# Product order, the steps of an attention pair, and who empties a plain bank, in a two-layer hybrid model

## The chip, the cores and the metric

The kernel runs on one core of one Trainium2 chip. The metric is the device time of one execution in microseconds, as the median of several runs. A core has five engines that matter here: PE (TensorE, matmuls into the eight PSUM banks), DVE (VectorE), ACT (ScalarE), POOL (GpSimd) and SP (SyncE, which here only issues DMAs). POOL too is used mostly to issue DMAs. Each engine works through its own instructions in their order, and waits for the others by semaphores.

## The reference, cut to what matters

512 tokens of width 1024 pass through two layers: dilated attention and a gated feed-forward block, then an mLSTM mixer and another feed-forward block. Only the attention is touched. It has three groups of query, key and value projections with 8 heads of 128; each group attends within windows of its own dilation, and the groups are joined by a softmax over their log-sums.

```python
proj = (xn @ w_in).reshape(B, S, N_GROUPS, 3, ATTN_HEADS, ATTN_HEAD_DIM)
for g, (window, dilation) in enumerate(((128, 1), (512, 4), (2048, 16))):
    q = apply_partial_rope(proj[:, :, g, 0], positions) * scale
    k = apply_partial_rope(proj[:, :, g, 1], positions)
    o, lse = dilated_window_attention(q, k, proj[:, :, g, 2], window, dilation)
wts = jax.nn.softmax(jnp.stack(lses), axis=0)
o = jnp.einsum('gbsh,gbshd->bshd', wts, jnp.stack(outs))
h = h + o.reshape(B, S, ATTN_WIDTH) @ w_out
```

## The kernel before, in words

All matmuls of projections are made in float32 by three products of rounded parts: an operand is split into a high part (ACT, `split_chunk`, L213) and a remainder (DVE subtraction, L214), and high times high, high times low and low times high are added up in a bank. A weight chunk of 128 x 1024 elements is loaded by SP into one of three raw buffers (`wraw`), split into one of four pairs of split buffers, and used by PE. `Feed` hands out the chunks in the order of a list, `plan`, and prepares three chunks ahead of the one that is being multiplied.

The heads are worked off in four **pairs**, pr = 0 to 3. While PE projects queries and keys of pair pr (`project_pair`), the attention of the pair before is done beside it. The names in the trace carry the pair first: a1g2 is group 2 of pair 1.

For pairs 1 to 3, group 0 is projected **plainly**: two chunks for the queries, two for the keys, each into two banks; `evac` (L948 to L961) empties a bank, with two ACT instructions that pack the 32 rows that rotation needs (L959) and a third that copies the whole bank (L961). For pair 0 the whole bank is emptied by DVE, which multiplies by the norm's factor (L952), and ACT packs from the copy (L956).

Groups 1 and 2 are projected together for queries and keys by a Strassen scheme (`qk_unit`): seven **products** P1 to P7 of half the size, each of 24 matmuls of 128 x 256, in the order of `ORDER`, which is also the order of the values in an earlier stage. They share three banks: P1 and P2 add up in c11, P5 and P3 in p5, and P6, P7 and P4 in u. After P1, ACT copies c11 into u (L878), and P6 adds to that. After P5 and after P6, ACT copies their bank into `vu` (L881, L883); P7 may add to u only when P6's copy has been taken. After P7 and P3, DVE adds bank and `vu` to the keys (L896); P4 may add to u only after P7's addition has read it. After P2 and P4, ACT packs and copies (L872, L890). P5, P6 and P7 need weight differences, which DVE makes (L845) in `prepare_part`; that function also starts the loads of the next group's weight quarters W11, W12, W21 and W22. After P4 the rotation of the group follows: a shuffle and three DVE passes (L593 to L602), and ACT copies back (L608 or L610), in group 1 one step later.

**Steps.** `advance` counts steps and runs what was put off until then (`defer`). Group 0 of a pair makes four steps (one for each chunk); each Strassen group makes four more, after its 2nd, 4th, 6th and 7th product. So in a pair steps 5 to 8 lie in group 1 and steps 9 to 12 in group 2. `RUN_AT` says at which steps of a pair the attention of the pair before is run:

```python
SCORES0_AT = 5
RUN_AT = (1, (4, 5, 6, 7, 8), (10, 11), (2, 3, 1))
```

- step 1: scores of groups 1 and 2 (`scores12`, L707) and their exponentials (L732);
- step 4: joint softmax factors and the first head's weighing (L777, L780), run in the middle of the last plain chunk;
- step 5: the first head's 32 x 32 transposition on DVE (L786) and its four stores to DRAM from POOL's queue (L789);
- step 6: the second head's weighing; step 7: its transposition and stores, and the first head's read-back (`bring`, L794, POOL's queue); step 8: the second head's read-back;
- steps 10 and 11: the two heads' weighted **values** (L804, L809), 30 matmuls each into one bank, which ACT copies (`keep_head`, L622) and POOL stores;
- steps 2, 3 and 1: the loads of the values from DRAM.

`SCORES0_AT` counts from the end of group 0 (step 4): so at step 9 the **first scores** of the new pair (`scores0`, L686) are computed, into two banks with the tag "s" for the first head and two with the tag "o" for the second; DVE adds the mask and takes the maxima (L692), which empties the banks, then exponentials follow on ACT (L726). Values needs a bank with the tag "o" as well, of which there are two. The probabilities and their transposed copies share four buffers (tag "p").

**What sets the order.** The framework plans each engine's order ahead of the run: an instruction traced earlier has priority, but one that the planner takes to be ready may pass another that it takes to be waiting. `run` keeps a block of matmuls together behind the PE instruction traced last and lets later ones follow it; `tc.issue_after(ins)` keeps all instructions of its block behind `ins` on that engine. Neither adds a semaphore.

Of the kernel before, what the change touches and what calls it, by code (L numbers as in the profile page):

```python
# [11 lines left out]
F32 = mybir.dt.float32  # L12
# [3 lines left out]
ALU = mybir.AluOpType  # L16
# [16 lines left out]
C1 = 6.28125  # L33
C2 = float(np.float32(np.uint32(np.float32(TWO_PI - C1).view(np.uint32) & 0xFFFFF000).view(np.float32)))
C3 = float(np.float32(TWO_PI - C1 - C2))
SCORES0_AT = 5
RUN_AT = (1, (4, 5, 6, 7, 8), (10, 11), (2, 3, 1))
LAST_AT = (1, (3, 3, 3, 3, 3), (), (1, 1, 1))
STACK_AT = (9, 11, 15, 17)
HEAD_AT = ((9, 10, 12), (10, 11, 13), (12, 13, 15), (13, 14, 16), (15, 16, 18), (16, 17, 19), (18, 19, 21),  # L40
# [33 lines left out]
def tile_hybrid_dilated_attn_mlstm(  # L74
# [127 lines left out]
        return raw, n, view, name  # L202

    spare = []
    splits = itertools.count()

    def split_chunk(chunk):

        raw, n, view, name = chunk
        p, more, bufs = (spare[0], "4", 1) if spare and next(splits) % (W_BUFS + 1) == W_BUFS else (wp, "", W_BUFS)  # L210
        hi = p.tile([P, 1024], F32R, tag="whi" + more, name=name + "_h", bufs=bufs)
        lo = p.tile([P, 1024], F32R, tag="wlo" + more, name=name + "_l", bufs=bufs)
        nc.scalar.activation(hi[:, :n], raw[:, :n], AF.Copy)  # L213
        nc.vector.tensor_tensor(lo[:, :n], raw[:, :n], hi[:, :n].bitcast(F32), op=ALU.subtract)  # L214
        return view(hi), view(lo)

    def split_weights(src, shape, name):
# [172 lines left out]
    with ExitStack() as actx:  # L390
# [249 lines left out]
        def attention_pair(pr, qks):  # L640
# [36 lines left out]
            def scores0(q, k):  # L677

                for i in range(2):
                    for b2 in range(2):  # L680
                        sp = score_bank(i, "%ss0" % nm)
                        o, parts = 0, []
                        for b in (2 * b2, 2 * b2 + 1):
                            lo_ = max(b - 1, 0) * P
                            w = (b + 1) * P - lo_
                            nc.tensor.matmul(sp[:, o:o + w], q[:, i, b * P:(b + 1) * P],  # L686
                                             k[:, i, lo_:lo_ + w], start=True, stop=True)
                            parts.append((b, o, w))
                            o += w
                        for b, o, w in parts:  # L690
                            pb = max(2 * b - 1, 0)
                            nc.vector.tensor_tensor_reduce(  # L692
                                p0[i][:, pb:pb + w // P, :].rearrange("p a b -> p (a b)"),
                                sp[:, o:o + w], mask_band[:, 2 * P - w:], 1.0, -3e38,
                                op0=ALU.add, op1=ALU.max, accum_out=own[:, 0, 0, i, b:b + 1])
                for i in range(2):
                    exponentials(0, i)

# [127 lines left out]

        postponed = []

        four_k = lambda t: t.rearrange("p (k n) -> p k n", k=4)
        parts_of = {}  # L830

# [9 lines left out]
        def prepare_part(pr, g, name):  # L841
            b = parts_of[pr, g]

            def less(out, x, y):
                nc.vector.tensor_tensor(b[out], b[x], b[y], op=ALU.subtract)  # L845
            src = {"P1": "W11", "P5": "W11", "P6": "W11", "P2": "W21", "P7": "W12", "P3": "W22", "P4": "W21"}[name]
            if name == "P5":
                less("W11", "W12", "W11")
            elif name == "P6":
                less("W11", "W22", "W11")  # L850
            elif name == "P7":
                less("W12", "W22", "W12")
            whl = split_chunk((b[src], 1024, four_k, "a%dg%d%s" % (pr, g, name)))
            if name == "P7":
                less("W21", "W21", "W11")
                for key in ("W11", "W12"):
                    load_part(pr, g + 1, key)
            elif name == "P4":
                for key in ("W21", "W22"):
                    load_part(pr, g + 1, key)  # L860
            return whl

        def qk_unit(pr, g, qk):
# [10 lines left out]
            def finish(name):  # L874
                nonlocal rot, vu
                if name == "P1":
                    acc["u"] = acc_tile(nm + "u")
                    nc.scalar.activation(acc["u"], acc["c11"], AF.Copy)  # L878
                elif name == "P5":
                    vu = ap.tile([P, 2, SEQ], F32, tag="vu", name=nm + "vu")  # L880
                    nc.scalar.activation(vu[:, 0], acc["p5"], AF.Copy)  # L881
                elif name == "P6":
                    nc.scalar.activation(vu[:, 1], acc["u"], AF.Copy)  # L883
                elif name in ("P2", "P4"):
                    th = int(name == "P4")
                    src = two_m(acc[target[name]])
                    if th == 0:
                        rot = ap.tile([P, 2, SEQ], F32, tag="rot", name="rot")
                    pack(th, src[:R])
                    nc.scalar.activation(halves(qk[0], th), src, AF.Copy)  # L890
                    if last and th:
                        rope(qk, rot, False, 1, 2, True)
                else:
                    th = int(name == "P7")
                    out = halves(qk[1], th)
                    nc.vector.tensor_tensor(out, two_m(acc[target[name]]), two_m(vu[:, 1 - th]), op=ALU.add)  # L896
                    pack(2 + th, out[:R])
                    if last and th == 0:
                        rope(qk, rot, False, 0, 1, True)
                        rope(qk, rot, False, 2, 4, True)  # L900

            for n, name in enumerate(ORDER):
                key = target[name]
                if name in ("P1", "P5"):
                    acc[key] = acc_tile(nm + key)
                whl = feed.pop()
                with fenced():
                    for m in range(2):
                        for k in range(4):
                            for a, b in SPLITS:  # L910
                                if name in ("P1", "P2", "P4"):
                                    x_ = pair[b][k + 4 * (name != "P1")][:, HALF * (name == "P4"):HALF * (1 + (name == "P4"))]
                                else:
                                    x_ = sum_part(name, b, k)
                                nc.tensor.matmul(acc[key][:, m * HALF:(m + 1) * HALF], whl[a][:, k, m * P:(m + 1) * P], x_,
                                                 start=(name in ("P1", "P5") and m == 0 and k == 0 and (a, b) == SPLITS[0]),
                                                 stop=(m == 1 and k == 3 and (a, b) == SPLITS[-1]), skip_group_check=True)
                finish(name)
                if n == 6 and not last:
                    back = rope(qk, rot, False)  # L920
                    if g == 2:
                        back()
                    else:
                        defer(1, back)
                if n in (1, 3, 5, 6):
                    advance()

        def project_pair(pr, qks, then=None):
            nm = "a%d" % pr
            for g in range(3):  # L930
# [14 lines left out]
                for part in range(2):  # L945
                    t = tok_tile("%sg%d_%s" % (nm, g, "qk"[part]))

                    def evac(m, acc, t=t, rot=rot, g=g, part=part):  # L948
                        to = rot()
                        views = (in_order, by_block) if g == 0 else (lambda x: x,) * 2  # L950
                        if pr == 0:
                            nc.vector.tensor_tensor(views[0](t[:, m]), views[1](acc), views[1](rbc), op=ALU.mult)  # L952
                        for th in range(2):
                            q = 2 * part + th
                            if pr == 0:
                                nc.scalar.activation(packed(to, q, m, g == 0),  # L956
                                                     turned((t, t), q, m, g == 0), AF.Copy)
                            else:
                                nc.scalar.activation(packed(to, q, m, False), acc[:R, th * HALF:(th + 1) * HALF], AF.Copy)  # L959
                        if pr:  # L960
                            nc.scalar.activation(views[0](t[:, m]), views[1](acc), AF.Copy)  # L961
                    if pr == 0 and g == 0 and part == 0:
                        def first_evac(evac=evac):
                            bc_hook()
# [212 lines left out]

        def last_plain(pr):
            whl = split_chunk(weight_chunk(w_in, 1, pr * 256 + D, 4, "a%dg0k_k1" % pr))
            for key in ("W11", "W12", "W21", "W22"):  # L1180
                load_part(pr, 1, key)
            return whl

# [2 lines left out]
        for pr in range(HEADS // 2):  # L1186
            for g, part, ch in itertools.product(range(3), range(2), range(2)):
                if pr and g:
                    if (part, ch) == (0, 0):
                        plan += [lambda pr=pr, g=g, name=name: prepare_part(pr, g, name) for name in ORDER]  # L1190
                elif pr and (part, ch) == (1, 1):
                    plan.append(lambda pr=pr: last_plain(pr))
                elif (pr, g) != (0, 0):
# [1141 lines left out]
```

## Time and profile before

| | |
|---|---|
| median of 3 runs | 1407.97 us (1407.84 to 1408.24) |
| the profiled execution | 1408.62 us |
| its span, first to last instruction | 1406.8 us |
| granted TensorE clock, mean of the span | 0.994 |
| PE busy | 1377.5 us, 98% |
| DVE busy | 1105.8 us, 79% |
| ACT busy | 803.7 us, 57% |
| PE busy in pair 1, 176.0 to 262.4 | 79.85 of 86.40 us |
| PE busy in pair 2, 262.4 to 344.4 | 79.85 of 82.00 us |
| PE busy in pair 3, 344.4 to 426.9 | 78.23 of 82.50 us |

In the profile, L214 is line 214 of the kernel; `a1g2u<-S3h,a1g2P_h` names what an instruction writes and reads, without buffer numbers. A row of the list of waits reads: who waited, for whom, the total in us, how many times, the longest. A row of the timeline reads: start, duration, engine, line, operation, names, shapes, count, and in brackets the engine's idle time before it and what ended it. A row of the table of stretches reads: the stretch, its length, busy time and instructions of PE, of its weight loads, DVE, ACT and POOL, the granted clock, the DMAs' share and GB/s. A row of the groups ends with busy time, mean ns of one, and idle time before them.

### The profile page before, as it was taken

What the parts mean: (1) busy time and instruction counts of PE and PEld (TensorE: products, weight loads), DVE (VectorE), ACT (ScalarE), POOL (GpSimd) and SP (SyncE); (2) the same over time, 40 slices, a digit from 0 to 9 for tenths busy, and PEclk for the clock granted to TensorE, in tenths of its full rate; (3) what the DMA queues carried; (4) which work ended last, traced back from release to release, by engine and by line L of the source; (5) the groups of instructions that cost most, each with busy time, mean ns of one, the idle gap of its engine ahead of it and who ended that gap; (6) DMA issues with size and microseconds to landing.
All of it is one profiled execution on the core that took longest, in us unless ns stands there. A gap on an engine that the chain in (4) does not pass through costs nothing. (4 is left out here: it accounts for less than half of the span.)

```text
span 1406.8 us, 22647 instructions
## 1 busy us (share of the span) xinstructions
PE 1377.5 (98%) x8740; PEld 1249.7 (89%) x8740; DVE 1105.8 (79%) x1841; ACT 803.7 (57%) x1346; POOL 163.1 (12%) x240
## 2 busy tenths in 40 slices
PE   9999998999999999999999999999999999999997
PEld 7888888899888788999999998888888899999886
DVE  7758668585877289878878888998858987887887
ACT  6556576566765155544466554786534544458854
POOL 3000011111011001000000101113101240001213
PEclk9999999999999999999999999999999999999999
DMA  8534247346275546432354652333334563335963
GB/s 286 181 120 135 92 138 227 121 132 217 65 240 152 170 128 161 132 121 74 107 168 95 145 149 75 93 91 99 97 120 111 131 201 121 120 106 130 199 165 98
DMA packets 140068, 193.82 MB, mean 138 GB/s; under 512 B 8980, under 2 KB 104788, under 8 KB 139960
## 3 DMA queue, kind: packets, MB, share of 16 engines
q1 hardware_dynamic: 119552, 139.81, 31.6%
q0 software_dynamic: 18752, 51.43, 15.9%
q8 instruction: 69, 1.13, 0.3%
q10 hardware_dynamic: 1656, 1.12, 0.2%
q14 instruction: 39, 0.32, 0.1%
HBM read 167.30 MB, written 22.54 MB: 135 GB/s over the span
## 5 line engine op out<-in xcount | busy, mean ns | idle before, releaser
L1638 POOL DMA_DIRECT2D f1T<-in_ffn_w_out_dram x15 | 17.8, 1186 | 208.8 <-DMA f1P_2w_w<-in_ffn_w_out_dram 136.4
L1613 POOL DMA_DIRECT2D f0S<-in_ffn_w_out_dram x10 | 8.7, 874 | 260.2 <-ACT f0P L1595 172.9
L2170 POOL DMA_DIRECT2D hD<-hB x32 | 21.7, 696 | 68.5 <-DVE hB L2167 68.5
L244 PE MATMUL mo<-n_h,mo_k_l 128*128 128x512 f32 x64 | 25.3, 396 | 0.0
L244 PE MATMUL mo<-n_h,mo_k_h 128*128 128x512 f32 x64 | 25.2, 394 | 0.0
L244 PE MATMUL mo<-n_l,mo_k_h 128*128 128x512 f32 x64 | 25.2, 394 | 0.0
L244 PE MATMUL awo<-ao_h,awo_k_h 128*128 128x512 f32 x64 | 25.2, 393 | 0.0
L244 PE MATMUL mwo<-yo_l,mwo_k_h 128*128 128x512 f32 x64 | 25.1, 393 | 0.0
L244 PE MATMUL mqk<-n_h,mqk_k_h 128*128 128x512 f32 x64 | 25.1, 392 | 0.0
L244 PE MATMUL awo<-ao_l,awo_k_h 128*128 128x512 f32 x64 | 25.1, 392 | 0.0
L244 PE MATMUL mqk<-n_l,mqk_k_h 128*128 128x512 f32 x64 | 25.1, 392 | 0.0
L244 PE MATMUL f0j<-n_h,f0j_h 128*128 128x512 f32 x64 | 25.0, 391 | 0.0
L244 PE MATMUL f1j<-n_h,f1j_h 128*128 128x512 f32 x64 | 25.0, 391 | 0.0
L244 PE MATMUL mwo<-yo_h,mwo_k_l 128*128 128x512 f32 x64 | 25.0, 391 | 0.0
L244 PE MATMUL mqk<-n_h,mqk_k_l 128*128 128x512 f32 x64 | 25.0, 390 | 0.0
L244 PE MATMUL awo<-ao_h,awo_k_l 128*128 128x512 f32 x64 | 25.0, 390 | 0.0
L244 PE MATMUL f0j<-n_h,f0j_l 128*128 128x512 f32 x64 | 24.9, 390 | 0.0
L244 PE MATMUL f1j<-n_h,f1j_l 128*128 128x512 f32 x64 | 24.9, 390 | 0.0
L244 PE MATMUL f0j<-n_l,f0j_h 128*128 128x512 f32 x64 | 24.9, 389 | 0.0
L244 PE MATMUL f1j<-n_l,f1j_h 128*128 128x512 f32 x64 | 24.9, 389 | 0.0
L244 PE MATMUL mwo<-yo_h,mwo_k_h 128*128 128x512 f32 x64 | 24.8, 391 | 0.0
L214 DVE TENSOR_TENSOR v1P_l<-v1W,v1P_h 128x1024 fp32r<-128x1024 f32 x14 | 17.1, 1223 | 9.3 <-ACT v1P_h L213 9.3
(2617 smaller groups left out, 5896.0 us busy)
## 6 DMA issues: line engine op xcount, KB each, us to landing
f0j_w<-in_ffn_w_in_dram SPq DMA_DIRECT2D x17, 512.0 KB, 5.9
f1j_w<-in_ffn_w_in_dram SPq DMA_DIRECT2D x17, 512.0 KB, 6.0
f1T<-in_ffn_w_out_dram POOLq DMA_DIRECT2D x15, 512.0 KB, 7.4
f0hid<-in_ffn_w_in_dram SPq DMA_DIRECT2D x9, 512.0 KB, 5.8
f1hid<-in_ffn_w_in_dram SPq DMA_DIRECT2D x9, 512.0 KB, 5.2
v0W<-in_attn_w_in_dram SPq DMA_DIRECT2D x8, 512.0 KB, 7.0
v1W<-in_attn_w_in_dram SPq DMA_DIRECT2D x8, 512.0 KB, 4.3
awo_k_w<-in_attn_w_out_dram SPq DMA_DIRECT2D x8, 512.0 KB, 7.1
```

Source lines behind the costliest of these rows:

```text
L214: nc.vector.tensor_tensor(lo[:, :n], raw[:, :n], hi[:, :n].bitcast(F32), op=ALU.subtract)
L244: nc.tensor.matmul(acc, whl[a][:, k, m * P:(m + 1) * P], pairs[b][kk], start=(kk == 0 and (a, b) == SPLITS[0]), stop=(kk == nk - 1 and (a, ...
L1613: nc.gpsimd.dma_start(t, src[1][:, ks], accum_op=ALU.add)
L1638: nc.gpsimd.dma_start(view(to), weight_rows(hk * UNITS + u, n), accum_op=ALU.add)
L2170: nc.gpsimd.dma_start(hD[k // 4].rearrange("(b i) x -> i b x", i=R)[:, :, c0:c0 + R], t[R * a_:R * (a_ + 1)])
```

## The change

1. The products of queries and keys are made in another order, `QK_ORDER`: P6 comes before P2. The values stage keeps `ORDER`. The half W22 of the next group is loaded after P3's split instead of with W21 after P4's.
2. The first scores run at step 10 instead of 9; the second head's weighing at 8 instead of 6, its transposition and the first read-back at 8 instead of 7, the second read-back at 9 instead of 8; values at 11 and 12 instead of 10 and 11. With the new order, step 9 lies after P5, step 10 after P2, step 11 after P3 and step 12 after P4.
3. A block `behind_scores` keeps every split remainder, weight difference and key addition that is traced after a pair's first scores behind the last of their reduces on DVE.
4. In pairs 1 to 3 a plain bank is emptied by one DVE copy, and ACT packs from that copy.

```diff
-SCORES0_AT = 5
-RUN_AT = (1, (4, 5, 6, 7, 8), (10, 11), (2, 3, 1))
+SCORES0_AT = 6
+RUN_AT = (1, (4, 5, 8, 8, 9), (11, 12), (2, 3, 1))
...
+    ahead_of_splits = [None]
+
+    def behind_scores():
+        return tc.issue_after(ahead_of_splits[0]) if ahead_of_splits[0] is not None else nullcontext()
...
         nc.scalar.activation(hi[:, :n], raw[:, :n], AF.Copy)
-        nc.vector.tensor_tensor(lo[:, :n], raw[:, :n], hi[:, :n].bitcast(F32), op=ALU.subtract)
+        with behind_scores():
+            nc.vector.tensor_tensor(lo[:, :n], raw[:, :n], hi[:, :n].bitcast(F32), op=ALU.subtract)
...
                                 op0=ALU.add, op1=ALU.max, accum_out=own[:, 0, 0, i, b:b + 1])
+                ahead_of_splits[0] = last_on(DVE)
                 for i in range(2):
                     exponentials(0, i)
...
+        QK_ORDER = ("P1", "P5", "P6", "P2", "P7", "P3", "P4")
...
             def less(out, x, y):
-                nc.vector.tensor_tensor(b[out], b[x], b[y], op=ALU.subtract)
+                with behind_scores():
+                    nc.vector.tensor_tensor(b[out], b[x], b[y], op=ALU.subtract)
...
-            elif name == "P4":
-                for key in ("W21", "W22"):
-                    load_part(pr, g + 1, key)
+            elif name in ("P3", "P4"):
+                load_part(pr, g + 1, src)
...
-                    nc.vector.tensor_tensor(out, two_m(acc[target[name]]), two_m(vu[:, 1 - th]), op=ALU.add)
+                    with behind_scores():
+                        nc.vector.tensor_tensor(out, two_m(acc[target[name]]), two_m(vu[:, 1 - th]), op=ALU.add)
...
-            for n, name in enumerate(ORDER):
+            for n, name in enumerate(QK_ORDER):
...
+                        else:
+                            nc.vector.tensor_copy(views[0](t[:, m]), views[1](acc))
                         for th in range(2):
                             q = 2 * part + th
-                            if pr == 0:
-                                nc.scalar.activation(packed(to, q, m, g == 0),
-                                                     turned((t, t), q, m, g == 0), AF.Copy)
-                            else:
-                                nc.scalar.activation(packed(to, q, m, False), acc[:R, th * HALF:(th + 1) * HALF], AF.Copy)
-                        if pr:
-                            nc.scalar.activation(views[0](t[:, m]), views[1](acc), AF.Copy)
+                            nc.scalar.activation(packed(to, q, m, g == 0), turned((t, t), q, m, g == 0), AF.Copy)
...
-            for key in ("W11", "W12", "W21", "W22"):
+            for key in ("W11", "W12", "W22", "W21"):
                 load_part(pr, 1, key)
...
-                        plan += [lambda pr=pr, g=g, name=name: prepare_part(pr, g, name) for name in ORDER]
+                        plan += [lambda pr=pr, g=g, name=name: prepare_part(pr, g, name) for name in QK_ORDER]
```

## The prediction

> **What bounds the kernel now.** I read the page first, then the list of waits on PE, then the stretches around the longest of them.
>
> ```profile
> span 1406.8 us, 22647 instructions
> PE 1377.5 (98%) x8740; PEld 1249.7 (89%) x8740; DVE 1105.8 (79%) x1841; ACT 803.7 (57%) x1346; POOL 163.1 (12%) x240
> ```
>
> PE is busy for 98% of the span. No edit takes a matmul away, so only PE's 29 us of idle time, and matmuls that run slowly, can be won. The list of PE's waits says where that time is:
>
> ```profile
> PE a0o L804 <- DVE a1own L692: 4.1, 1, 4.1
> PE a2o L804 <- DVE a3own L692: 3.2, 1, 3.2
> PE a3o L804 <- DMA a3pT<-a3pD: 2.5, 1, 2.5
> PE a1g1u L915 <- ACT a1g1vu L883: 1.5, 1, 1.5
> ...
> PE a1o L804 <- DVE a2own L692: 1.2, 1, 1.2
> PE a3g1u L915 <- ACT a3g1vu L883: 1.1, 1, 1.1
> ...
> PE a2g1u L915 <- ACT a2g1vu L883: 0.9, 1, 0.9
> PE a1g0k L244 <- ACT a1g_q L961: 0.9, 1, 0.9
> ```
>
> Seven of these eight lie in the stage that the diff edits, three kinds of them. **Values** (a0o, a1o, a2o): 4.1 + 3.2 + 1.2 = 8.5 us in which the first head's weighted values wait until DVE has reduced the next pair's first scores (L692). **P7** (a1g1u, a2g1u, a3g1u): 1.5 + 1.1 + 0.9 = 3.5 us in which P7 waits for ACT to copy P6's bank away. **Bank** (a1g0k): 0.9 us for a plain bank that ACT empties. The a3o wait is outside the diff.
>
> A wait also costs time after it. The stretches of the three values blocks of pairs 0 to 2, each behind its wait, with PEclk, the granted clock, in the column before the last two:
>
> ```profile
> 247.58:253.33 5.75, 5.75 (x31) 5.75 (x31) 0.84 (x6) 3.83 (x16) 0.00 (x0) 0.56 0.21 74
> 328.92:332.30 3.38, 3.37 (x30) 3.37 (x31) 1.94 (x7) 2.88 (x12) 0.00 (x0) 1.00 0.45 148
> 409.89:414.74 4.85, 4.84 (x30) 4.84 (x31) 2.53 (x8) 3.83 (x16) 0.00 (x0) 0.68 0.88 307
> ```
>
> The same work takes 3.38 us at clock 1.00 behind the 1.2 us wait, but 5.75 and 4.85 us at 0.56 and 0.68 behind the waits of 4.1 and 3.2. So shortening the two long waits also gives back 5.75 - 3.38 = 2.37 and 4.85 - 3.38 = 1.47 us, 3.8 together. [...]
>
> Why does DVE reduce so late? In pair 1 PE computed these scores from 234.55 on; DVE, in order of time:
>
> ```profile
> 234.55 3.20 PE L686 MATMUL a1s<-a1g_k,a1g_q 128*128 128x128 f32 x16
> ```
> ```profile
> 241.63 1.23 DVE L214 TENSOR_TENSOR a1g2P_l<-a1g2W,a1g2P_h 128x1024 fp32r<-128x1024 f32 x1 [0.95 <-ACT a1g2P_h L213]
> 244.50 1.23 DVE L214 TENSOR_TENSOR a2g0q_k_l<-a2g0q_k_w,a2g0q_k_h 128x1024 fp32r<-128x1024 f32 x1 [1.65 <-ACT a2g0q_k_h L213]
> 245.65 0.28 DVE L692 CUSTOM_DVE_ANT_0 a1p<-a1s,acst 128x128 f32<-128x128 f32 x1
> ...
> 248.13 0.29 DVE L721 TENSOR_SCALAR a1nb<-a1own 128x4 f32<-128x4 f32 x2
> ```
>
> The scores were there by 237.8, the reduces ran from 245.65 to 248.1. Right ahead of them stand weight splits (L214), for the last two of which DVE itself idles 0.95 and 1.65 us: each needs ACT's half, and that needs a weight buffer which PE frees only with a later product. DVE works in order, so 2.5 us of reduces stood for 8 us behind work that nobody needed yet.
>
> **The change part by part.**
>
> *The gate (issue_after), with scores one step and values one step later.* A split traced after the scores may no longer pass their reduces. The scores move from behind P5 to behind P2, two products later; of the splits in that stretch only P7's, P3's and P4's are then traced ahead of them, and the four weight buffers let P4's run once P6, before the scores, is multiplied. So DVE reaches the reduces about when the scores land and needs 248.1 - 245.65 = 2.5 us; values stands P7 + P3 = 5.8 us behind the scores. The 8.5 us go, and the 3.8 of clock. Queued behind the gate on DVE are the splits of the next pair's first chunk (PE needs them only after P4 and both values blocks, over 10 us later) and P7's add (P4, which waits for it, has P3 and a values block in front): zero. What is late next is the transfer of the probabilities, below.
>
> *Product order.* P6 moves ahead of P2, so P2's 24 matmuls stand between P6 and P7.
>
> ```profile
> 218.34 0.28 PE L915 MATMUL a1g1p<-S4h,a1g1P_h 128*128 128x256 f32 x1
> ...
> 218.97 0.28 PE L915 MATMUL a1g1p<-S4h,a1g1P_l 128*128 128x256 f32 x1
> 220.78 0.39 PE L915 MATMUL a1g1u<-S3h,a1g1P_h 128*128 128x256 f32 x1 [1.54 <-ACT a1g1vu L883]
> ```
>
> Now P6, the fourth product, ends at 218.34, where the first six matmuls of P3 were put ahead of the waiting P7; they start about 0.12 us apart, so a product of 24 takes 2.88. The rows also show that a wait costs 0.15 more than its idle time: 1.81 from start to start against 0.12 is 1.69 lost for 1.54 shown. Seven waits make 1.1 us. ACT in the same stretch, and the same two places in pair 2:
>
> ```profile
> 210.76 0.58 ACT L878 ACTIVATE a1g1u<-a1g1c 128x512 f32<-128x512 f32 x1
> ...
> 215.29 1.46 ACT L608 ACTIVATE a1g_q<-rot 32x256 f32<-32x256 f32 x4 [1.08 <-DVE rot L602]
> 216.76 1.46 ACT L608 ACTIVATE a1g_k<-rot 32x256 f32<-32x256 f32 x4
> ```
> ```profile
> 300.94 1.46 ACT L608 ACTIVATE a2g_k<-rot 32x256 f32<-32x256 f32 x4
> ```
> ```profile
> 303.13 0.28 PE L915 MATMUL a2g1p<-S4h,a2g1P_h 128*128 128x256 f32 x1
> ```
>
> P7 stays the fifth product, due at 218.3. P6 now ends at 215.5, but on ACT the copy of its bank stands behind eight rotation copies that end at 218.22 and takes 0.58, as L878 does: 218.8. That leaves some 0.6 us with the start-up. In pair 2 the copies end at 302.4, so P7's bank is free at 303.0, and it is due at 303.1: zero, and the same for pair 3. P6 itself needs L878's copy, done at 211.34, and is due at 218.3 - 5.76 = 212.6: zero (if that copy slips behind one 1.06 us split, still about zero). P4 must wait for P7's add on DVE and has P3's 2.88 us:
>
> ```profile
> 223.19 2.17 DVE L786 STREAM_TRANSPOSE a0pB<-a0p 128x1920 f32<-128x1920 f32 x1
> 225.29 0.65 DVE L896 TENSOR_TENSOR a1g_k<-a1g1u,a1g1vu 128x512 f32<-128x512 f32 x1
> ```
>
> Behind a whole transposition the add ends 2.17 + 0.65 = 2.82 after P7: nothing lost; with a 1.23 us split as well, 1.2 us. I take 0.3 in each pair, 0.9. The second half's load moves on SP from P4 to P3, one product earlier, with the need: zero.
>
> *Second head's weighing and transposition two steps later, its transfers one.* These feed the transfers that values needs. POOL's issues now, a matmul of P3 beside them, and from the view of the tile how long its transfers take to land:
>
> ```profile
> 225.66 2.18 POOL L789 DMA_DIRECT2D a0pD<-a0pB  x4 [5.80 <-DVE a0pB L786]
> 227.83 0.56 POOL L794 DMA_DIRECT2D a0pT<-a0pD  x1
> ```
> ```profile
> 223.76 0.28 PE L915 MATMUL a1g1p<-S4h,a1g1P_h 128*128 128x256 f32 x1
> ```
> ```profile
> DMA to landing us min/median/max: 6.8/8.0/9.2
> ```
>
> The first head's read-back is queued behind the second head's four stores and lands by 227.83 + 9.2 = 237.0. PE ran dry at 243.5 (the block starts at 247.58 behind 4.1 idle); with P7 and P3 moved ahead (+5.8) and the waits of a1g0k and P7 gone (-2.8), values is due at 246.5, so the slack is 9.5 us. The weighing moves by two steps, which are three products, 8.6 us: even if all behind it moves as far, the transfer lands in time; with the rotation's four DVE passes (2.8 us) in front as well it would cost 1.9 us in pair 1. I expect less: step 7, which traced the transposition, lay behind P3, and P3 had 18 matmuls to go at 223.76, when the transposition ran already (223.19). DVE works off what is ready, before its step too. I take zero. The second head's values slide only past P4; its bank is stored while the next chunk multiplies.
>
> *Plain banks by VectorE.*
>
> ```profile
> L961 ACT ACTIVATE a1g_q<-a1g0q 128x512 f32<-128x512 f32 x2 | 1.2, 599 | 0.0
> L952 DVE TENSOR_TENSOR a0g_k<-a0g0k,xrbc 128x512 f32<-128x512 f32 x2 | 1.4, 686 | 0.5 <-PE a0g0k L244 0.5
> ```
> ```profile
> 197.33 0.16 DVE L734 TENSOR_TENSOR a0own<-a0dn 128x4 f32<-128x4 f32 x1 [2.93 <-ACT a0p L732]
> ```
>
> Twelve copies of 0.60 us leave ACT and twelve join DVE; the trace has no such copy, the nearest row is 0.69 us for a multiplication out of a bank in the same layout, 8.3 us in all. The wait arose since ACT worked on exponentials (L732) until 197.3; DVE idled 2.93 us for the same exponentials. The 0.9 us go. The 8.3 us lie beside products; where DVE is full they cost at most 0.69 in front of a late split, and I take zero. [...]
>
> **The sum.** Gains: 8.5 + 3.8 + 3.5 + 0.9 + 1.1 = 17.8 us. Costs: 0.6 + 0.9 = 1.5. The profiled execution took 1408.62 us (span 1406.8 and 1.8 around it), 0.65 above the median of the runs, 1407.97. 1408.62 - 16.3 = 1392.3, against the median **1391.7**.
>
> **Rivals.**
>
> 1. *The gate holds only half.* Values still waits about as a1o does, because P4's split, waiting for its buffer, stays ahead of the reduces. For: splits ahead of reduces is today's fault and three remain allowed. Against: P4's buffer is freed before the scores. Three waits of 1.2 + 0.15 cost 4 us, with no clock loss: 1396. If nothing of the values wait goes, only 3.5 + 0.9 + 0.6 - 1.5 = 3.5 us are won: 1404.5.
>
> 2. *Nothing to measure*: the waits return under other names, P4 behind P7's add and values behind its transfer, for 16 us: 1408.
>
> 3. *Slower: the second head's transposition slips.* If DVE gets to the second head's weighing only when it meets the new scores, which PE ends at 246.5 - 5.8 = 240.7, its transposition ends near 244, POOL's four stores take until 246.6, the read-back lands at about 255.8, and values waits 9.3 us plus 2.4 at the low clock. Three pairs: 35.1 us in place of 8.5 + 3.8 + 0.5 = 12.8, 5.0 won elsewhere, 1.5 of costs: 1427. It decides once the transposition ends about 12 us later than now (9.5 of slack, then a wait of 2.9, which with 2.4 of clock eats a third of the 16.3). Against: it needs only the softmax factors, and did not wait for its step before.
>
> **Chances.** Forecast (1389 to 1395.5) 0.70; half gate (to 1405) 0.15; nothing 0.05; slower 0.10. A measurement of this kernel tells 0.2%, 2.8 us, from no change. Faster 0.85, same 0.05, slower 0.10. The range runs from 1389, all 17.8 and a little of a3o, to 1400, which takes in rival 1's first form and the unknown costs of P4 and the transfer.
>
> **What would show it.** The waits on L692 and on L883 are gone from PE's list, and so is the one on L961; the three values blocks take 3.4 us at clock 1.00; L692 starts within 2 us of the scores. New PE waits on L896 would be P4, on a0pT the transfer, on L878 P6. I am wrong if a values block still waits 3 us or more, since clock goes with it, or if L786 of the second head ends behind L692.

## The result, and the profile after

The changed kernel takes 1398.7 us (median of 4 runs, 1398.08 to 1400.34) against 1407.9 us beside it: a ratio of 0.9938, 95% interval 0.9921 to 0.9956. That is 0.6% faster, clear of the noise and inside the stated range to 1400, but beyond the forecast's own 1389 to 1395.5: 9.2 us were won where 16.3 were forecast. The profiled execution took 1398.08 us, its span 1396.3. In the kernel after, line numbers are 5 to 8 higher: the reduces are L697, the split remainder L219, the weight difference L853, the copy of P6's bank L890, P7's and P3's additions L904, group 0's rotation copies L613; in the experiments some shift by a few lines more.

PE's waits in the kernel after (who waited, for whom, total, times, longest):

```profile
PE a3o L810 <- DMA a3pT<-a3pD: 2.4, 1, 2.4
PE a2g1u L923 <- ACT a2g1vu L890: 2.1, 1, 2.1
PE a3g1u L923 <- ACT a3g1vu L890: 2.1, 1, 2.1
...
PE a3s L713 <- DVE a3g_q L604: 1.0, 1, 1.0
...
PE a1g1u L923 <- ACT a1g1vu L890: 0.8, 1, 0.8
PE a3g12v L331 <- ACT a3g_q L897: 0.7, 1, 0.7
PE a3xps L751 <- DVE a3ex L746: 0.6, 1, 0.6
PE a2g2p L923 <- ACT a2g_q L897: 0.6, 1, 0.6
```

The three values waits and the bank wait of a1g0k are gone, as forecast: in pair 1 the reduces now start at 241.88, 1.0 us behind the end of the scores (237.67 + 3.20), where they stood 8 us behind it before.

```profile
237.67 3.20 PE L691 MATMUL a1s<-a1g_k,a1g_q 128*128 128x128 f32 x16
241.88 0.28 DVE L697 CUSTOM_DVE_ANT_0 a1p<-a1s,acst 128x128 f32<-128x128 f32 x1
```

The P7 waits are not gone: 0.76 + 2.08 + 2.07 = 4.9 us, where there were 3.5 and 0.6 was expected. Four small waits are new: group 2's P5 of pair 2 for the copy of P4's bank (a2g2p), and three in pair 3 (a3s, a3g12v, a3xps). The stretches, PEclk ahead of the last two columns: the values blocks of pairs 0 to 2, P7 of pairs 2 and 3, and the last values block (a3o).

```profile
246.45:249.71 3.26, 3.26 (x32) 3.26 (x31) 2.89 (x4) 1.43 (x3) 0.00 (x0) 1.00 0.53 146
325.82:329.08 3.26, 3.26 (x32) 3.26 (x31) 0.41 (x1) 1.11 (x2) 0.00 (x0) 1.00 0.84 276
405.83:409.10 3.27, 3.27 (x33) 3.27 (x31) 1.44 (x3) 0.00 (x0) 0.00 (x0) 1.00 1.04 370
295.98:299.13 3.15, 3.15 (x26) 3.15 (x27) 2.93 (x3) 2.94 (x4) 2.18 (x4) 1.00 0.90 191
375.33:379.73 4.40, 4.40 (x25) 4.40 (x26) 4.18 (x5) 2.93 (x4) 2.19 (x4) 0.66 0.84 175
466.06:469.40 3.34, 3.34 (x30) 3.34 (x31) 0.00 (x0) 0.00 (x0) 0.00 (x0) 1.00 0.86 335
```

All values blocks run at a granted clock of 1.00. Pair 3's P7 loses 4.40 - 3.15 = 1.25 us at 0.66. The a3o block was slow in the kernel before, at 0.66:

```profile
474.45:479.43 4.98, 4.98 (x31) 4.98 (x31) 0.00 (x0) 0.00 (x0) 0.00 (x0) 0.66 0.56 215
```

So 4.98 - 3.34 = 1.64 us of the gain come from a wait that the diff doesn't touch and that hardly changed (2.5 to 2.4).

**Why P7 waits.** ACT in pair 2, in order of time:

```profile
292.53 1.46 ACT L613 ACTIVATE a2g_q<-rot 32x256 f32<-32x256 f32 x4 [2.86 <-DVE rot L607]
294.00 1.45 ACT L613 ACTIVATE a2g_k<-rot 32x256 f32<-32x256 f32 x4
295.36 0.57 ACT L890 ACTIVATE a2g1vu<-a2g1u 128x512 f32<-128x512 f32 x1
```

Group 1 starts (P1) at 282.19, so P7 was due 4 x 2.88 us later at 293.7; P6's bank is copied by 295.93, P7 starts at 295.98. The eight rotation copies stand in front, as the prediction had it, but they start 10.34 us after P1 (292.53 - 282.19), against 7.85 before (299.47 - 291.62). They wait for the rotation's last pass on DVE (L607). DVE ahead of it:

```profile
282.53 0.68 DVE L962 COPY a2g_k<-a2g0k 128x512 f32<-128x512 f32 x1
...
284.22 0.68 DVE L962 COPY a2g_k<-a2g0k 128x512 f32<-128x512 f32 x1
285.22 1.23 DVE L219 TENSOR_TENSOR a2g1P_l<-a2g1W,a2g1P_h 128x1024 fp32r<-128x1024 f32 x1 [0.32 <-ACT a2g1P_h L217]
...
287.26 1.22 DVE L853 TENSOR_TENSOR a2g1W<-a2g1W,a2g1W 128x1024 f32<-128x1024 f32 x1
...
290.76 1.13 DVE L786 TENSOR_SCALAR a1p<-a1p,a1cf 128x256 f32<-128x256 f32 x4
291.81 0.69 DVE L607 TENSOR_TENSOR rot<-rot 128x512 f32<-128x512 f32 x1
```

Two of the new bank copies now stand in this stretch, and weighing ends only at 291.9. Already before the change DVE had no gaps to take them: from P1's start to the end of group 1, the table of stretches has, for pairs 2 and 3 of the kernel before, DVE (the third busy time, behind PE and PE's weight loads) at 22.12 of 22.30 and 22.15 of 22.43 us.

```profile
291.62:313.92 22.30, 21.36 (x177) 21.12 (x176) 22.12 (x39) 15.18 (x25) 4.93 (x9) 1.00 0.64 177
370.45:392.88 22.43, 21.35 (x177) 21.09 (x176) 22.15 (x39) 15.17 (x26) 4.95 (x9) 1.00 0.62 175
```

### The profile page after: what moved, and what is told of

Same layout as the page of the kernel before. It is cut to its first block, busy times and chain, and to the rows that moved or that the text cites. A ratio compares the mean times of both kernels' runs of the same rounds, so it can differ in the third digit from the quotient of the medians.

```text
span 1396.3 us, 22650 instructions
## 1 busy us (share of the span) xinstructions
PE 1372.7 (98%) x8740; PEld 1245.1 (89%) x8740; DVE 1110.8 (80%) x1853; ACT 797.5 (57%) x1334; POOL 163.2 (12%) x240
## 3 DMA queue, kind: packets, MB, share of 16 engines
q8 instruction: 69, 1.13, 0.3%
## 5 line engine op out<-in xcount | busy, mean ns | idle before, releaser
L219 DVE TENSOR_TENSOR v1P_l<-v1W,v1P_h 128x1024 fp32r<-128x1024 f32 x14 | 17.1, 1224 | 9.3 <-ACT v1P_h L217 9.3
```

## The experiments

Each kernel was timed beside the kernel before; "ratio" is to that, and since the kernel before took 1407.15 to 1408.16 us from round to round, the ratios compare better than the medians. Rotation: us from P1's start to the start of group 0's first rotation copy in pair 2 (7.85 in the kernel before).

| kernel | median us | ratio, 95% interval | rotation |
|---|---|---|---|
| after | 1398.70 | 0.9938, 0.9921 to 0.9956 | 10.34 |
| no_gate | 1418.58 | 1.0075, 1.0061 to 1.0088 | |
| gate_only | 1396.69 | 0.9927, 0.9915 to 0.9939 | |
| steps_gate | 1393.97 | 0.9897, 0.9884 to 0.9910 | 7.92 |
| order_old | 1394.15 | 0.9905, 0.9891 to 0.9918 | 8.45 |
| banks_act | 1396.25 | 0.9923, 0.9909 to 0.9936 | 9.46 |
| back_late | 1391.95 | 0.9891, 0.9878 to 0.9905 | |
| fill_late | 1391.91 | 0.9892, 0.9879 to 0.9905 | |
| copies_first | 1401.07 | 0.9948, 0.9936 to 0.9961 | |
| order_back | 1408.77 | 1.0014, 1.0003 to 1.0026 | |
| p6_first | 1392.79 | 0.9894, 0.9880 to 0.9907 | |
| no_weigh0 | 1387.41 | 0.9857, 0.9845 to 0.9870 | 7.47 |
| no_p6_diff | 1399.94 | 0.9943, 0.9928 to 0.9958 | 9.45 |

**The gate.** Without it:

```diff
     def behind_scores():
-        return tc.issue_after(ahead_of_splits[0]) if ahead_of_splits[0] is not None else nullcontext()
+        return nullcontext()
```

> The kernel after, but the block behind_scores orders nothing, so weight splits, weight differences and P7's addition may pass the first scores' reduces on DVE again. Theory (the gate is what ended the values waits): the values waits on the reduces return, some 2 to 4 us each in three pairs, with 1 to 2.4 us of low clock behind the long ones, so 1405 to 1412 us. Rival (the scores one step and the values one step later suffice alone): values still starts without a wait, within 1 us of the kernel after, 1398 to 1400 us.

```profile
PE a2o L810 <- DVE a3own L697: 7.7, 1, 7.7
PE a1o L810 <- DVE a2own L697: 5.8, 1, 5.8
PE a0o L810 <- DVE a1own L697: 5.5, 1, 5.5
```

The theory, and more: 19.0 us of values waits, where there were 8.5 before. The rest of the change without its gate is slower than the kernel before: with this order and these copies, the later steps don't suffice. (The steps by themselves were not run.) And the gate alone, in the kernel before (the diff's `behind_scores` lines and nothing else):

> The kernel before with the block behind_scores alone: scores, values, weighing, product order and banks are at their old places. Theory (the gate alone ends the values waits, the later steps only make room): the 8.5 us of waits and most of the 3.8 us of low clock go: 1395 to 1398 us. Rival (scores and values must also come later, since at the old step the splits of P2, P6 and P7 are still traced ahead of the reduces): values waits of 1 to 3 us stay in each pair: 1400 to 1406 us.

It takes 1396.69 us, as the theory had it, and the intervals can't tell it from the whole change. Two values waits are gone; the third stays, as the rival had it for all:

```profile
PE a2o L810 <- DVE a3own L697: 2.5, 1, 2.5
```

**Gate and steps, without order and bank copies.** The product order and loads of before (first diff), and ACT's copies of the plain banks (second):

```diff
-        QK_ORDER = ("P1", "P5", "P6", "P2", "P7", "P3", "P4")
+        QK_ORDER = ("P1", "P5", "P2", "P6", "P7", "P3", "P4")
...
-            elif name in ("P3", "P4"):
-                load_part(pr, g + 1, src)
+            elif name == "P4":
+                for key in ("W21", "W22"):
+                    load_part(pr, g + 1, key)
...
-            for key in ("W11", "W12", "W22", "W21"):
+            for key in ("W11", "W12", "W21", "W22"):
                 load_part(pr, 1, key)
```

```diff
-                        else:
-                            nc.vector.tensor_copy(views[0](t[:, m]), views[1](acc))
...
+                            if pr == 0:
...
+                            else:
+                                nc.scalar.activation(packed(to, q, m, False), acc[:R, th * HALF:(th + 1) * HALF], AF.Copy)
+                        if pr:
+                            nc.scalar.activation(views[0](t[:, m]), views[1](acc), AF.Copy)
```

Second diff alone:

> The kernel after, but ACT empties the plain banks as before. Theory T1 (the twelve DVE copies are what pushed joint factors, weighing and rotation back on DVE, so that group 0's eight rotation copies stand on ACT in front of the copy of P6's bank): the P7 waits of pairs 2 and 3 fall from 2.1 us to under 0.8, 2.5 to 4 us are won there with their clock loss, the 0.9 us wait for a1g0k's bank returns: 1394.5 to 1396.5 us. Rival T2 (the new product order does it, because P6's weight difference and split now come earlier): P7 keeps its 2 us and the bank wait comes on top: 1399 to 1400 us.

First diff alone:

> The kernel after, but queries' and keys' products in the order P1 P5 P2 P6 P7 P3 P4, and the half W22 loaded behind P4 as before; steps, gate and DVE copies of the banks stay. T1 (the DVE copies push the rotation back): P7 follows P6 at once and still waits for the copy of P6's bank, 1 to 3 us in each pair, 4 to 8 together: 1398 to 1403 us. T2 (the product order pushes the rotation back): the rotation copies are done before P6's copy, as in the kernel before, and the P7 waits are those of before, 3.5 us together: 1396 to 1398 us.

Both:

> The kernel after with the old product order and with ACT emptying the plain banks: what is left of the change are the gate and the steps. If the losses found so far for the new order (4.5 us) and for the DVE copies (2.5 us) stand beside each other: 1391 to 1392.5 us, with P7 waits like those of the kernel before, 3 to 4 us together, and the 0.9 us for a1g0k's bank. If both are the same loss, seen twice (the rotation copies late on ACT): 1394 to 1396 us.

With after these make a square. Old order: 1393.97 us (ACT's copies) and 1394.15 (DVE's); new order: 1396.25 and 1398.70. By these medians the new order costs 2.3 us with ACT's copies and 4.5 with DVE's, and the DVE copies cost 0.2 in the old order and 2.5 in the new. But steps_gate comes from a round in which the kernel before took 1407.15, and the other two from one in which it took 1408.16. By the ratios the order costs 3.7 and 4.6 us, the copies 1.1 and 2.1. The intervals separate the two corners of the old order from after; new order with ACT's copies they separate neither from after nor from steps_gate. So gate and steps alone are faster than the whole change; that the order loses time is shown with DVE's copies, and whether the copies lose time, and whether the two losses are one, the times don't tell.

The traces say more. The rotation comes 0.5 to 0.9 us later by the DVE copies, 1.5 to 1.9 by the order, 2.4 by both, so neither T1 nor T2 holds alone. order_old came out better than either expected; one new wait, of 1.1 us for a split of P3 (a1g1p), stands beside its P7 waits. The new order takes the wait between P6 and P7 away only when the rotation is early enough. In banks_act it isn't quite, but P7 no longer waits, since P5 has waited already:

```profile
281.12 1.06 ACT L217 ACTIVATE a2g1P_h<-a2g1W 128x1024 fp32r<-128x1024 f32 x1 [2.61 <-DVE a2g1W L853]
...
284.37 1.04 ACT L217 ACTIVATE a2g1P_h<-a2g1W 128x1024 fp32r<-128x1024 f32 x1
...
286.20 0.60 ACT L969 ACTIVATE a2g_k<-a2g0k 128x512 f32<-128x512 f32 x1
```

In the new order P5's and P6's weights follow each other in one buffer, W11: ACT stands 2.61 us for a difference on DVE, and the plain banks behind its splits are copied late (P5, due 2.88 us after P1's 282.92, starts at 286.85). In order_old, where P7 follows P6, 3.4 us of P7 waits stay, and the rotation copies aren't next in front of P6's copy:

```profile
292.51 1.45 ACT L613 ACTIVATE a2g_k<-rot 32x256 f32<-32x256 f32 x4
293.99 1.06 ACT L217 ACTIVATE a2g1P_h<-a2g1W 128x1024 fp32r<-128x1024 f32 x1
294.95 0.57 ACT L880 ACTIVATE rot<-a2g1c 32x512 f32<-32x512 f32 x1
295.43 0.57 ACT L898 ACTIVATE a2g_q<-a2g1c 128x512 f32<-128x512 f32 x1
295.91 0.57 ACT L891 ACTIVATE a2g1vu<-a2g1u 128x512 f32<-128x512 f32 x1
```

They end at 294.0, about when P6 ends too (P3 follows at 294.07); a split and the two copies of P2's bank stand between them and P6's copy, which ends at 296.48, 2.4 us behind P6. Those three come behind the rotation copies in ACT's order, though, so that these still push them; order_back, below, tests it.

**The rotation copies behind P6's bank copy** (new order, DVE copies):

```diff
                 finish(name)
+                if name == "P6":
+                    while rotated:
+                        behind(rotated.pop(0), engine=ACT)
...
+                        elif pr:
+                            rotated.append(turn())
                         else:
                             defer(1, turn())
```

> The kernel after, but group 0's eight rotation copies on ACT are kept behind the copy of P6's bank. All theories in which those copies are what P7 waits for: the P7 waits of 0.8, 2.1 and 2.1 us go, with 7 x 0.15 less and some 1.3 us of low clock behind the one in pair 3: 1392 to 1393.5 us. Rival (P6's copy is late for another reason, its bank or vu not being free): P7 still waits about 2 us in pairs 2 and 3: 1398 to 1399 us. Second rival (the copies are needed soon themselves): the first scores wait for the copied queries and keys instead, 1398 us or more.

All P7 waits go, with the small waits at the end of pair 3: 1391.95 us. That this is within 0.3 us of the forecast for the whole change is chance: the kernel has an edit more. That the rotation copies are what P7 waits for is shown. Two other waits appear:

```profile
PE a1g2p L924 <- ACT a1g_q L898: 2.3, 1, 2.3
PE a3g2p L924 <- ACT a3g_q L898: 1.5, 1, 1.5
```

```profile
226.89 2.00 ACT L217 ACTIVATE a1g2P_h<-a1g2W 128x1024 fp32r<-128x1024 f32 x2 [1.93 <-DMA a1g2W<-in_attn_w_in_dram]
...
229.53 0.60 ACT L898 ACTIVATE a1g_q<-a1g1u 128x512 f32<-128x512 f32 x1
```

ACT stands before a split whose weights are still under way (W21, for group 2's fourth product), with the copy that frees P5's bank behind it.

**Those splits behind the copies of P4's bank:**

```diff
+                late = g == 1 and n == 6
+                feed.ahead -= late
+                with tc.issue_after(copied.pop()) if copied else nullcontext():
+                    whl = feed.pop()
...
+                if late:
+                    feed.ahead += 1
+                    copied.append(last_on(ACT))
+                    behind(feed.fill, engine=ACT)
```

> The kernel with group 0's rotation copies behind P6's bank copy, and in addition ACT's halves of group 2's splits for P6 and P2 kept behind ACT's copies of P4's bank in group 1. Theory (in pairs 1 and 3 ACT stands in order before the split of the quarter W21, whose load has not landed, while P4's copies, for which group 2's P5 waits, are ready behind it): the waits of 2.3 us (a1g2p) and 1.5 us (a3g2p) go and pair 2, where that split already stood behind the copies, doesn't change: 1387 to 1389 us. Rival (the weight itself is late and only the name of the wait changes): PE waits as long, for P6's or P2's split in group 2: 1391 to 1393 us.

Both waits go, as the theory said, and the time stays, as the rival said (1391.91): in pair 2, whose order on ACT is unchanged, P4 now waits for P7's addition, in a stretch in which DVE works 21.53 of 21.95 us.

```profile
PE a2g1u L931 <- DVE a2g_k L909: 1.2, 1, 1.2
...
PE a3g2u L931 <- DVE a3g2P_l L219: 0.6, 1, 0.6
```

```profile
281.99:303.94 21.95, 20.72 (x171) 20.42 (x170) 21.53 (x46) 14.68 (x26) 2.19 (x4) 1.00 0.47 133
```

**In addition ACT's copies of the plain banks**, with P2's split behind the last of them (`copied.append(last_on(ACT))` behind the keys' part):

> The kernel with rotation copies behind P6's bank copy and group 2's splits behind P4's copies, in which in addition ACT empties the plain banks as before and ACT's half of P2's split stays behind the last of those copies. Theory (ACT holds finished banks behind splits that nobody needs yet, and the DVE copies fill a VectorE that is full in group 1): the waits for P7's addition in pair 2 (1.2 us) and for group 2's P6 (0.5 and 0.6 us) shrink, and P5 doesn't wait for the plain bank: 1388.5 to 1390.5 us. Rival (the time lost is handed on to the next wait in a full VectorE): within 1 us of the kernels it is made from, 1391 to 1393 us.

A miss, 1401.07 us. DVE no longer makes these copies, but now stands before P6's difference in group 2, whose load W22 is late, with P3's addition behind it; group 2's P5 waits 2.2 us for what follows, and runs slowly after it (clock 0.59):

```profile
306.63 1.23 DVE L858 TENSOR_TENSOR a2g2W<-a2g2W,a2g2W 128x1024 f32<-128x1024 f32 x1 [1.99 <-DMA a2g2W<-in_attn_w_in_dram]
...
308.91 0.68 DVE L909 TENSOR_TENSOR a2g_k<-a2g1p,a2g1vu 128x512 f32<-128x512 f32 x1
```

```profile
311.52:315.50 3.98, 3.98 (x21) 3.98 (x22) 3.98 (x5) 3.29 (x4) 2.39 (x5) 0.59 0.31 62
```

**The old order with the rotation copies behind P6's copy** (the diffs of order_old and back_late together):

> The kernel after with the old product order, and group 0's rotation copies behind P6's bank copy. Theory (with P7 right behind P6 its wait is the copy of P6's bank itself, which stands behind ACT's two copies of P2's bank, and not the rotation copies, which end 2 us earlier): the P7 waits stay at 1 to 1.6 us in pairs 2 and 3: 1393 to 1394.5 us. Rival (the rotation copies hold ACT up there too): the P7 waits fall below 0.7 us: 1391 to 1392 us.

A miss in time by either theory: 1408.77 us. But the P7 waits go, as the rival had it: the rotation copies do hold ACT up in the old order too. P6's bank is now copied 1.6 us behind P6's end (at 297.02, where P3 follows P6 at 295.39) instead of 2.4, and PE has more of P3 to work on meanwhile. P7's addition, however, now stands on DVE behind a difference that waits 3.38 us for its load, and P4 waits 4.4 and 4.9 us for the addition:

```profile
305.27 1.23 DVE L854 TENSOR_TENSOR a2g2W<-a2g2W,a2g2W 128x1024 f32<-128x1024 f32 x1 [3.38 <-DMA a2g2W<-in_attn_w_in_dram]
306.41 0.68 DVE L906 TENSOR_TENSOR a2g_k<-a2g1u,a2g1vu 128x512 f32<-128x512 f32 x1
```

**Steps and gate alone, with P6's copy ahead of P2's two** on ACT:

```diff
-                whl = feed.pop()
+                with tc.issue_after(copied.pop()) if copied else nullcontext():
+                    whl = feed.pop()
...
-                finish(name)
+                if name != "P2":
+                    finish(name)
+                if name == "P6":
+                    copied.append(last_on(ACT))
+                    behind(finish, "P2", engine=ACT)
```

> Gate and steps alone (old product order, ACT empties the plain banks), with ACT's copy of P6's bank kept ahead of its two copies of P2's bank and of the split of group 2's P1. Theory (in the old order those three instructions, 2.2 us on ACT, are what makes P7 wait behind P6): the P7 waits of 1.0 to 1.6 us fall below 0.5 us in each pair, 3 to 3.5 us in all: 1390.5 to 1391.5 us. Rival (P7's wait is the copy itself behind the end of P6, and is handed on to P4's wait for the addition): 1393 us or more.

The P7 waits fall from 3.6 to 0.8 us together; P4's wait for the addition takes part of it, twice 0.5 us. 1392.79 us can't be told from steps_gate.

**Load or chain?** Two kernels leave work out of DVE ahead of the rotation; they don't compute the whole attention and serve only to see which waits go. Without the first head's weighing:

```diff
                 joint()
-                weigh(0)
```

> The kernel after without the first head's weighing (eight DVE instructions, 2.1 us in each pair, leave the stretch ahead of the rotation's last addition; the first head's probabilities stay unweighted). Theory L (in group 1 VectorE has no time left, so that any 2 us of its work there reach the end of the rotation, and with it the copy of P6's bank): the P7 waits of 2.1 us in pairs 2 and 3 go almost whole: 1392.5 to 1395 us. Theory C (what is late is the chain through the buffer W11, P5's split, then P6's difference, then P6's split, whatever else VectorE has to do): P7 waits 1.5 us or more, 1397 to 1399 us.

Without P6's difference:

```diff
-            elif name == "P6":
-                less("W11", "W22", "W11")
```

> The kernel after without P6's weight difference in groups 1 and 2 of pairs 1 to 3 (P6 multiplies by P5's weights; six DVE instructions of 1.22 us leave, and ACT's split for P6 no longer waits for one). Theory C (the new order puts P6's difference and split right behind P5's split, through one buffer, and ACT's and VectorE's copies of the plain banks, joint factors and weighing queue up behind them): most of what the order costs beside the DVE copies, 4.5 us, comes back: 1393.5 to 1396 us. Theory L (only the load counts): 1.22 us less work in front of the rotation, 2 to 2.4 us in two pairs together: 1396 to 1397 us. If neither: 1398 us or more.

Both agree with theory L. In no_weigh0 the rotation starts 2.9 us earlier for 2.2 us of work less (1.07 + 1.13), every P7 wait is gone, and with them pair 3's small waits and, since pair 3 isn't weighed either, a3o's; hence 1387.41, below what was expected, although a new wait of 1.6 us (a1g2p) appears. Group 1 then takes 20.29 us in pair 2, seven products of 2.88 plus 0.1, and DVE is at 19.85 even so:

```profile
283.59:303.88 20.29, 20.29 (x171) 20.29 (x170) 19.85 (x32) 13.55 (x24) 2.18 (x4) 1.00 0.65 197
```

In no_p6_diff it starts 0.9 us earlier for 1.22 less: no more than the load explains, so nothing calls for a chain of its own. P7 waits 0.3 us in pairs 2 and 3, but P5 waits 0.7 there. Its total tells nothing of that, since pair 3 lost the gain elsewhere:

```profile
402.54 1.06 ACT L217 ACTIVATE a3g12v_k_h<-a3g12v_k_w 128x1024 fp32r<-128x1024 f32 x1 [6.41 <-DMA a3g12v_k_w<-in_attn_w_in_dram]
403.50 0.57 ACT L877 ACTIVATE rot<-a3g2c 32x512 f32<-32x512 f32 x1
```

ACT stood 6.41 us before a split whose load was late, the rotation's input behind it, and the reduces behind the rotation on DVE: a2o waited 5.0 us. The kernel after has such a stand too, with the first scores' exponentials behind it on ACT, and its waits of a3g12v, a3s and a3xps come after that; that they come from it was not tried:

```profile
409.97 1.06 ACT L217 ACTIVATE a3g12v_k_h<-a3g12v_k_w 128x1024 fp32r<-128x1024 f32 x1 [7.42 <-DMA a3g12v_k_w<-in_attn_w_in_dram]
```

Why this load lands late in some of the kernels was not tried and stays open.

## Why the prediction was right in sign and too large

- **Values and clock** (8.5 + 3.8): right. All three waits are gone, and the two slow blocks gave 2.49 + 1.58 = 4.1. no_gate shows that the gate does it; gate_only that the steps are needed for pair 2's block alone. That the time lies where the half-gate rival put it (up to 1405) doesn't bear that rival out: no values block waits.
- **Bank** (0.9): right, the wait is gone.
- **Transposition and transfer** (0): right in price, wrong in reason, and so luck. I expected less displacement than the steps. Counted from group 1's start, the second head's transposition came 8.4 us later than before in pair 1 (229.50 - 204.76 against 223.19 - 206.80) and 12.3 and 12.7 in pairs 2 and 3, there more than the 8.6 that I took as the bound and more than the slack of 9.5. It cost nothing because the first head's read-back, which the sum and the slower rival had queued behind the second head's four stores, now leaves POOL ahead of them, in pair 1 at 226.04, and in pairs 2 and 3 likewise (305.16 and 384.19, the stores at 312.20 and 392.12):

```profile
226.04 0.56 POOL L800 DMA_DIRECT2D a0pT<-a0pD  x1 [6.66 <-ACT rot L879]
231.97 2.19 POOL L795 DMA_DIRECT2D a0pD<-a0pB  x4 [5.37 <-DVE a0pB L792]
238.78 0.56 POOL L800 DMA_DIRECT2D a0pT<-a0pD  x1 [4.62 <-DMA a0pD<-a0pB]
```

- **P4** (0.9) and **P6** (0): P4 cost nothing, no wait on L904 is in the list.
- **P7** (3.5 won, 0.6 left): the step that failed. "In pair 2 the copies end at 302.4, so P7's bank is free at 303.0, and it is due at 303.1" took the copies' end from the kernel before, as if the change left their place alone. In pair 2 they came 2.5 us later after P1 than before, and P7 was due at the same distance; only pair 1, where 0.6 was forecast and 0.8 measured, came out. Measured in all: 4.9 us of waits and three start-ups of 0.15 instead of 0.6, and 1.25 us of clock, 6.0 us too much together. back_late shows that these copies are what P7 waits for, and no_weigh0 that DVE's load in group 1 makes them late; nothing in no_p6_diff calls for a chain through one buffer besides. The product order, expected to win these 3.5 us, lost time.
- **DVE copies**: "The 8.3 us lie beside products; where DVE is full they cost at most 0.69 in front of a late split, and I take zero." Rows of the kernel before speak against it: DVE at 22.1 of 22.3 us in group 1. The two copies that fall there, 1.4 us, put the rotation off by 0.5 and 0.9 us. Such a copy takes 0.68 us in the kernel after (L962).
- **W22's load** ("with the need: zero"): wrong. P6's difference for group 2 waits 0.62 us for it in pair 2 of the kernel after, ACT's split for P6 waits 1.27 us for that difference, and the copy for which a2g2p waits 0.6 us stands behind the split.
- **Not in the sum**: a2g2p and pair 3's three waits, 2.9 us and 0.6 of start-ups; in return a3o's clock (1.6), 0.1 of its wait, a pair 1 that began 0.8 earlier (178.91 against 179.69), 0.9 not spent on P4 and 0.3 more clock, 3.7. None of these gains was forecast, and why a3o's block ran at a clock of 1.00 and pair 1 began earlier stays open.

6.0 + 3.5 - 3.7 = 5.8 us, which is 1398.08 - 1392.3. It closes less well than it looks: 10.0 of the 10.5 us won lie ahead of the end of the a3o block (479.43 - 469.40), the other 0.5 behind it, outside the stage that was edited. And that the time still lies in the range to 1400 is partly luck: the range was left open for a half-held gate, P4 and the transfer, none of which cost anything, and 1.6 us of a3o's clock came in unforeseen.

steps_gate, order_old, back_late, fill_late and p6_first beat both kernels, after by 4.5 to 7 us; of the kernels that do the whole work none came below the forecast, 1391.7.

## What to carry to other kernels

Before an instruction is moved to an engine or ahead of others there, read that engine's share in the very stretch where it will stand: DVE, at 79% of the span, was at 99% in group 1 (22.12 of 22.30 us), and what it released next came later, by 0.5 to 0.9 us for 1.4 us of added work. In an order fixed ahead, an instruction that waited for a load or for another engine held everything behind it: the gate won 10 us by keeping such work behind what PE needs (gate_only, ratio 0.9927), and copies_first, order_back and no_p6_diff lost time to the next instruction of that kind, before which DVE stood 1.99 and 3.38 us and ACT 6.41 us. When a wait is removed, put the new places of all its neighbours into the sum, not the old ones.

## What the hardware showed that was not expected

The granted clock fell behind some waits of about 2 us and not behind others of the same length: 2.07 us (a3g1u) was followed by 0.66, 2.08 (a2g1u) by 1.00, 2.2 in copies_first by 0.59, and a3o's 2.4 by 1.00 after, its 2.5 by 0.66 before. What decides between them was not shown. So in this kernel a term for the clock behind a wait of 2 us is a chance, not a sum.
